# A transformer block on one core: the last of seven products moved to the free half of another PSUM bank, and two matmuls of the down projection cut in two

## The chip, the cores and the metric

The kernel runs on one core of a Trainium2 chip. A core has a matrix engine (TensorE; PE in the profile, and PEld for its weight loads), a vector engine (VectorE, DVE), a scalar engine (ScalarE, ACT), GpSimd (POOL), and the queue that issues most DMAs (SyncE, SP). Matmul results go to PSUM, eight banks of 512 float32 columns on 128 partitions; everything else on the chip lives in SBUF. The metric is the device time of one launch in microseconds.

## The reference

One layer of a hybrid encoder block over 512 positions of width 1024, in float32: an attention mixer with two head groups, a cross-attention into 256 memory tokens, and a SwiGLU feed-forward layer, each with an RMSNorm before and after. The change touches the feed-forward layer alone:

```
D_MODEL = 1024; SEQ = 512; D_FF = 2816

def swiglu(h, w_gate_up, w_down):
    g, u = jnp.split(h @ w_gate_up, 2, axis=-1)
    return (jax.nn.silu(g) * u) @ w_down
...
h = rms_norm(x, g_ffn_pre[l])
x = x + rms_norm(swiglu(h, w_gate_up[l], w_down[l]), g_ffn_post[l])
```

## The kernel before

**Three matmuls for one.** Each float32 operand is held as a high part and a low part. A product of two of them is three matmuls (`mm3`, lines 140 to 142): high by high, high by low, low by high. Each matmul has a weight load of its own, 128 rows by 128 columns, in front of it. The moving operand is 256 or 512 columns wide; in this text a 256-column matmul is one whose moving operand has 256 columns.

**Gate and up.** The 2816 columns of gate and of up are worked in blocks of 256 columns, alternately one of gate and one of up. There are 22 blocks; the first two are done with the end of cross-attention, and 20 follow in the loop over `u`. Three of these 20 multiply in the plain way (`eight`, 96 matmuls). The other 17 use a scheme in the manner of Strassen and Winograd: seven products of half-size blocks and some additions in place of eight products (`seven`, line 1116). One product (`product`, line 1063) is 4 times `mm3`, 12 matmuls of 256 columns, so a block of seven has 84 matmuls. All 256-column work of this stage forms one unbroken sequence on PE.

A block of seven takes four PSUM banks, called `p17`, `p26`, `p35` and `p4`. Gate blocks take three banks of the group "a" and the one bank "o"; up blocks take two banks "s" and two "t". A half bank (`left` or `right`, 256 columns) holds one product. In order, the seven products go to p17 left, p26 right, p35 left, p26 left, p4 left, p17 right and, once more, p26 left. VectorE combines them into `O` (the tile `G` for gate, `U` for up): line 1128 reads both halves of p26 after the fourth product, line 1129 reads p35, line 1134 reads p17 right, line 1135 reads p4 left, and line 1138 reads the seventh product. The seventh product overwrites p26 left, which line 1128 has to have read by then.

**Weights.** The weights arrive by DMA in tiles `fraw` (three buffers). VectorE adds blocks of them (`sums`, lines 929 to 932), ScalarE writes the high part into a ring (`ring_hi`, line 902), and VectorE writes the low part (`ring_lo`, line 903). The ring has two places for the first item of a block of seven and three for the other three items (`single`, `double`); `take` fills a place as soon as the products that used it are written down in the program. All of this and the combining of products share VectorE's and ScalarE's queues, whose order a scheduler fixes when the program is built.

**Down projection.** The output is worked in two halves of 512 columns (`half`). Four of the eleven blocks of the hidden dimension (`SEVEN`) are again done with seven products (`seven_products`, line 1242): 42 matmuls of 256 columns each, 168 in a row for the four blocks. The other blocks (`down`, line 1223) are matmuls of 512 columns. In half 0 the order is four blocks of 512 columns, the 168 matmuls of 256 columns, and blocks of 512 columns; in half 1 it is one block of 512 columns, the 168, and the rest. So each half has one 256-column stretch that begins and ends between 512-column matmuls. `mm` (line 1218) sends each operand pair to `mm3`.

Of the kernel before, what the change touches and what calls it, by code (L numbers as in the profile page):

```python
# [11 lines left out]
ALU = mybir.AluOpType  # L12
AX = mybir.AxisListType

P = 128
SEQ = 512
D = 1024
NT = SEQ // P
# [18 lines left out]
def hybrid_block_kernel(  # L37
# [20 lines left out]
    act, dve, pool, pe = nc.scalar, nc.vector, nc.gpsimd, nc.tensor  # L58
# [12 lines left out]
    def f32(ap):  # L71
        return ap.bitcast(F32)
# [66 lines left out]
    def mm3(dst, sh, sl, mh, ml, first, last):  # L139
        pe.matmul(dst, sh, mh, start=first, stop=False)  # L140
        pe.matmul(dst, sh, ml, start=False, stop=False)  # L141
        pe.matmul(dst, sl, mh, start=False, stop=last)  # L142
# [84 lines left out]
    with tc.tile_pool(name="mix", bufs=1, reuse_waits="tile") as bp:  # L227
# [114 lines left out]
        for t in range(NT):  # L342
# [3 lines left out]
                out=z[:, t, :], in0=acc0[t][:, 256:264], scalar=r, in1=gn[:, B_F : B_F + 8],  # L346
# [34 lines left out]
        for b in range(3):  # L381
            l = bp.tile([P, 2, SEQ], F32R, tag=f"L{b}", name=f"L{b}")
# [261 lines left out]
    with tc.tile_pool(name="cross", bufs=1, reuse_waits="tile") as cp:  # L644
# [12 lines left out]
        def quarter(name, dtype=F32R):  # L657
            serial[0] += 1
            return cp.tile([P, 1024], dtype, tag="q", name=f"{name}{serial[0]}", bufs=8)
# [5 lines left out]
        with later(-115):  # L665
            for c in range(4):
                hi, lo = unit()
                acc = bank("a")
                for b in range(2):
# [9 lines left out]
                    out=kT[:, 1, 2 * c : 2 * c + 2, :], in0=a3,  # L679
                    in1=f32(kT[:, 0, 2 * c : 2 * c + 2, :]), op=ALU.subtract,  # L680
# [4 lines left out]
        for half in range(2):  # L685
            hi, lo = unit()
            for t in range(NT):
                acc = bank("a")
                for k in range(4):
# [5 lines left out]
                    out=m, in0=acc, scalar=rs_g[1][:, t : t + 1], in1=m, op0=ALU.mult, op1=ALU.add  # L695
# [3 lines left out]
                if half:  # L699
                    r = small(1, "prs")  # L700
                    dve.scalar_tensor_tensor(
                        out=r, in0=mix_ms[:, 0, t : t + 1], scalar=EPS, in1=mix_ms[:, 1, t : t + 1],
# [4 lines left out]
                        out=mix[:, t, :], in0=mix[:, t, :], scalar=r, in1=xo[t], op0=ALU.mult, op1=ALU.add  # L707
# [35 lines left out]
        for h in range(4):  # L743
            for o in (oTh, oTl):
                t = quarter("oT").rearrange("p (k n) -> p k n", k=2)
                o += [t[:, 0], t[:, 1]]
        for h in range(4):
            hi, lo = unit()
            q = qq[:, h % 2]
            for b in range(2):  # L750
                acc = bank("a")
                cs = slice(b * P, (b + 1) * P)
                for k in range(KB):
# [3 lines left out]
                    out=q[:, 1, b, :], in0=acc, scalar=1.0 / 16.0, in1=f32(q[:, 0, b, :]),  # L757
# [3 lines left out]
            for i in range(0, NT, 2):  # L761
                s = bank("s")
                for j in range(2):
# [8 lines left out]
                    out=nm, in_=s.rearrange("p (j n) -> p j n", j=2), axis=AX.X, op=ALU.max, negate=True  # L772
# [9 lines left out]
                for j in range(2):  # L782
                    dve.tensor_scalar(
                        out=p[:, i + j, :], in0=p[:, i + j, :], scalar1=rs[:, j : j + 1],
# [11 lines left out]
            for b in range(2):  # L796
                acc = bank("o")
                cs = slice((2 * h + b) * P, (2 * h + b + 1) * P)
                for k in range(2):
# [6 lines left out]
                    out=oTl[2 * h + b], in0=acc, in1=f32(oTh[2 * h + b]), op=ALU.subtract  # L806
# [146 lines left out]
        SEVEN = (4, 5, 6, 7)  # L953
        DOWN = ((0, 1, 2, 3, 4, 5, 6, 7, 8, 9, 10), (0, 4, 5, 6, 7, 1, 2, 3, 8, 9, 10))
# [108 lines left out]
        def product(dst, w, b, first=True, last=True):  # L1063
            for k in range(4):
                mm3(dst, w[0][:, k, :], w[1][:, k, :], b[:, 0, k, :], b[:, 1, k, :], first and k == 0, last and k == 3)

        left, right = slice(0, 256), slice(256, 512)
# [22 lines left out]
        for b in range(2):  # L1090
# [5 lines left out]
        t1, t2, t3, t4 = (  # L1096
            wp.tile([P, 2, 4, 256], F32R, tag=tag, name=f"t{tag}", bufs=2) for tag in ("hi", "hi", "lo", "lo")
        )
# [14 lines left out]
        def twice(a):  # L1113
            return bass.AP(a.tensor, a.offset, [list(a.ap[0]), [0, 2], list(a.ap[-1])])

        def seven(O, tags, done):

            p17, p26, p35, p4 = (bank(tag) for tag in tags)
            v = cp.tile([P, 256], F32, tag="v", name="v", bufs=2)
            (a11,) = take()  # L1120
            product(p17[:, left], a11, b11)
            act.copy(v, p17[:, left])
            ((h, l),) = take()
            product(p26[:, right], (h[:, 0], l[:, 0]), t2)
            product(p35[:, left], (h[:, 1], l[:, 1]), b22)
            ((h, l),) = take()
            product(p26[:, left], (h[:, 0], l[:, 0]), b21)
            dve.tensor_tensor(out=O[:, 0], in0=halves(p26), in1=twice(v), op=ALU.add)
            dve.tensor_tensor(out=O[:, 1, 0], in0=p35[:, left], in1=O[:, 0, 1], op=ALU.add)
            done(0, 0)  # L1130
            product(p4[:, left], (h[:, 1], l[:, 1]), t4)
            ((h, l),) = take()
            product(p17[:, right], (h[:, 0], l[:, 0]), t3)
            dve.tensor_tensor(out=O[:, 1, 1], in0=p17[:, right], in1=O[:, 0, 1], op=ALU.add)
            dve.tensor_tensor(out=O[:, 0, 1], in0=p4[:, left], in1=O[:, 1, 1], op=ALU.add)
            done(0, 1)
            product(p26[:, left], (h[:, 1], l[:, 1]), t1)
            dve.tensor_tensor(out=O[:, 1], in0=twice(p26[:, left]), in1=O[:, 1], op=ALU.add)
            done(1, 0)
            done(1, 1)  # L1140

# [14 lines left out]
        for u in range(1, FB // 2):  # L1156
# [4 lines left out]
            dst = hidden(u)  # L1161
# [49 lines left out]
        for half, tail in enumerate((2, 3)):  # L1211
# [3 lines left out]
            p1, p5, p7, p6 = (bank(tag) for tag in (("s", "s", "t", "t"), ("a", "a", "a", "o"))[half])  # L1215
            begun = set()

            def mm(bank_, to, lhs, rhs, end=False):
                first = id(bank_) not in begun
                begun.add(id(bank_))  # L1220
                mm3(bank_[:, to], lhs[0], lhs[1], rhs[0], rhs[1], first, end)

            def down(t, i, w, end=False, parts=(slice(0, 512),)):
                ts = slice(t * P, (t + 1) * P)
                for to in parts:
                    for j in range(2):
                        k = 2 * i + j
                        mm(
                            accs[t], to, (gh[k][:, ts], gl[k][:, ts]), (w[0][:, j, to], w[1][:, j, to]),
                            end and j == 1 and to is parts[-1],  # L1230
                        )
# [10 lines left out]
            def seven_products(u, last):  # L1242
                (w,) = take()
                block(p1, u, 0, w, 0, last)
                block((0, 0), u, 1, w, 1)
                block((0, 1), u, 5, w, 2)
                (w,) = take()
                block(p5, u, 6, w, 0, last)
                block(p7, u, 4, w, 1, last)
                block(p6, u, 3, w, 3, last)  # L1250
                block((2, 0), u, 2, w, 2)
# [13 lines left out]
            body = DOWN[half][: FB // 2 - tail]  # L1265
            for i in body:
                if i in SEVEN:
                    seven_products(i, i == SEVEN[-1])
                    if half == 0 and i == SEVEN[0]:
                        spare = cp.tile([P, 4160], F32R, tag="vm", name="latev")  # L1270
                        late(8, spare)
                        late(9, spare[:, 2048:])
                    if half == 0 and i == SEVEN[1]:
                        late(10, cp.tile([P, 2112], F32R, tag="pt", name="latep"))
                    if i == SEVEN[-1]:
                        gather()
                    continue
                (w,) = take()
                if half == 0 and i < 4:
                    late_seven(SEVEN[i])  # L1280
                for t in range(NT):
                    down(t, i, w)
            ends = take(tail)
            for t in range(NT):
# [11 lines left out]
                else:  # L1296
# [8 lines left out]
                    for hf in range(2):  # L1305
                        c2 = slice(hf * 512, (hf + 1) * 512)
                        dve.scalar_tensor_tensor(
                            out=yd[:, t, c2], in0=(yd[:, t, c2], gained)[hf], scalar=r, in1=xr[:, t, c2],
# [58 lines left out]
```

## Time and profile before

| | |
|---|---|
| median of three runs | 787.18 us (786.44 to 787.55) |
| the profiled execution | 786.29 us, of which the span of the trace is 783.9 us |
| granted clock of PE | 0.998 of full speed |
| PE busy | 763.0 us of 783.9 |
| DVE busy | 592.1 us |
| ACT busy | 426.7 us |
| gate and up, from the first ring weights to the down projection | 462.5 to 660.5 us |
| 256-column stretch of down, half 0 | 682.2 to 702.0 us |
| 256-column stretch of down, half 1 | 723.8 to 743.6 us |

The profile takes one execution. The record of one matmul overlaps those of its neighbours, since matmuls are pipelined; how fast PE goes is read from the distance of their starts. The two microseconds and a half between span and time lie outside the trace.

### The profile page before, as it was taken

Reading aid. Unit: us, or ns where it says so; the run is one execution under the profiler, and the core shown is the slowest. Engines: PE = TensorE matmul, PEld = TensorE weight load, DVE = VectorE, ACT = ScalarE, POOL = GpSimd, SP = SyncE. Lnnn points to the kernel's source line nnn. Section 1 sums busy time; section 2 is a strip of 40 time slices with the busy share of each in tenths; the row PEclk is TensorE's granted clock in tenths of the full one; section 3 lists DMA queues with packets and bytes.
Section 4 is the critical chain, followed back from the end, with each engine's and each line's share of the span. In section 5 each row is a group of like instructions: output and inputs, shape, how many; then the busy total and the mean of one; then the engine's idle time right before and its main releaser. Section 6 shows DMA issues by size and latency. Waiting matters only on the chain.

```text
span 783.9 us, 12757 instructions
## 1 busy us (share of the span) xinstructions
PE 763.0 (97%) x4958; PEld 679.9 (87%) x4958; DVE 592.1 (76%) x1073; ACT 426.7 (54%) x774; POOL 70.8 (9%) x110
## 2 busy tenths in 40 slices
PE   8999999999999999999999999999999999999996
PEld 8887788888778888877778899999999999898985
DVE  6567889879887588545663778998899999986626
ACT  7358888757875348444553635545354446543411
POOL 6001231110321101000001100000000000000001
PEclk9999999999999999999999999999999999999999
DMA  7342112422322724421350202332433332241402
GB/s 245 83 132 55 54 55 68 137 68 78 109 68 90 275 106 162 133 75 60 108 174 15 81 28 81 108 109 81 135 109 108 108 110 105 84 159 57 138 23 108
DMA packets 60747, 80.04 MB, mean 102 GB/s; under 512 B 2704, under 2 KB 43664, under 8 KB 60688
## 3 DMA queue, kind: packets, MB, share of 16 engines
q1 hardware_dynamic: 59264, 74.49, 29.4%
q0 software_dynamic: 1280, 4.72, 1.8%
q8 instruction: 39, 0.64, 0.3%
q14 instruction: 20, 0.16, 0.1%
q10 hardware_dynamic: 144, 0.02, 0.0%
HBM read 77.13 MB, written 2.10 MB: 101 GB/s over the span
## 4 chain that ended last, share of the span: by engine, by line
PE 73%; DVE 11%; ACT 6%; issue 4%; DMA 3%; POOL 2%; SPq 0%; DVEq 0%; POOLq 0%; ACTq 0%
PE ps_a L141 14%; PE ps_a L142 14%; PE ps_a L140 14%; PE ps_s L140 4%; PE ps_s L141 4%; PE ps_s L142 4%; DVE ring_lo L903 3%; PE ps_t L534 2%; DMA raw<-in_dram 2%; PE ps_t L141 2%; PE ps_t L140 2%; PE ps_t L142 2%; PE ps_o L543 2%; PE ps_o L140 1%; PE ps_s L515 1%
## 5 line engine op out<-in xcount | busy, mean ns | idle before, releaser
L902 ACT CAST ring_hi<-fraw 128x1024 fp32r<-128x1024 f32 (+1 forms) x62 | 57.5, 932 | 64.6 <-PE ps_t L142 17.6
L126 DVE TENSOR_TENSOR lo<-raw,hi 128x1024 fp32r<-128x1024 f32 x56 | 68.2, 1223 | 22.2 <-ACT hi L125 21.9
L903 DVE TENSOR_TENSOR ring_lo<-fraw,ring_hi 128x1024 fp32r<-128x1024 f32 (+1 forms) x62 | 66.4, 1074 | 21.7 <-ACT ring_hi L902 21.5
L142 PE MATMUL ps_a<-hTh,lo 128*128 128x512 f32 x192 | 76.8, 400 | 0.6 <-DVE lo L126 0.6
L140 PE MATMUL ps_a<-hTh,hi 128*128 128x512 f32 x192 | 75.9, 395 | 0.2 <-ACT hi L125 0.2
L141 PE MATMUL ps_a<-hTl,hi 128*128 128x512 f32 x192 | 76.0, 396 | 0.0
L125 ACT CAST hi<-raw 128x1024 fp32r<-128x1024 f32 x56 | 57.8, 1048 | 24.0 <-PE ps_a L141 15.2
L902 ACT CAST ring_hi<-sums 128x1024 fp32r<-128x1024 f32 x34 | 35.7, 1050 | 48.7 <-PE ps_a L141 20.0
L903 DVE TENSOR_TENSOR ring_lo<-sums,ring_hi 128x1024 fp32r<-128x1024 f32 x34 | 41.4, 1219 | 3.4 <-ACT ring_hi L902 3.4
L142 PEld LDWEIGHTS ps_a<-hTh,lo 128*128 128x128 f32 x192 | 36.1, 188 | 7.3 <-DVE lo L126 1.0
L141 PEld LDWEIGHTS ps_a<-hTl,hi 128*128 128x128 f32 x192 | 36.1, 188 | 6.4
L140 PEld LDWEIGHTS ps_a<-hTh,hi 128*128 128x128 f32 x192 | 36.2, 188 | 6.1 <-ACT hi L125 0.4
L529 ACT ACTIVATE p<-p,nm 128x128 f32<-128x128 f32 (+1 forms) x64 | 36.1, 564 | 8.4 <-DVE nm L519 7.6
L140 PE MATMUL ps_a<-b,ring_hi 128*128 128x256 f32 x140 | 39.0, 279 | 0.0
L141 PE MATMUL ps_a<-b,ring_hi 128*128 128x256 f32 x140 | 38.9, 278 | 0.0
L142 PE MATMUL ps_a<-b,ring_lo 128*128 128x256 f32 x140 | 38.9, 278 | 0.0
L140 PE MATMUL ps_s<-b,ring_hi 128*128 128x256 f32 x128 | 35.6, 278 | 0.0
L141 PE MATMUL ps_s<-b,ring_hi 128*128 128x256 f32 x128 | 35.6, 278 | 0.0
L142 PE MATMUL ps_s<-b,ring_lo 128*128 128x256 f32 x128 | 35.6, 278 | 0.0
L536 ACT CAST pth<-ps_t 128x128 fp32r<-128x128 f32 (+1 forms) x64 | 27.1, 425 | 14.6 <-PE ps_t L534 13.8
L537 DVE TENSOR_TENSOR ptl<-ps_t,pth 128x128 fp32r<-128x128 f32 (+1 forms) x64 | 30.7, 486 | 5.0 <-ACT pth L536 3.6
L534 PE MATMUL ps_t<-ident,p 128*128 128x128 f32 x160 | 28.1, 275 | 1.1 <-DVE p L531 0.8
(528 smaller groups left out, 2618.0 us busy)
## 6 DMA issues: line engine op xcount, KB each, us to landing
raw<-in_dram SPq DMA_DIRECT2D x64, 512.0 KB, 3.7
fraw<-in_dram SPq DMA_DIRECT2D x62, 512.0 KB, 3.5
cb<-in_dram SPq DMA_DIRECT2D x8, 256.0 KB, 2.6
xo<-in_dram POOLq DMA_DIRECT2D x4, 512.0 KB, 5.3
out_dram<-yd SPq DMA_DIRECT2D x8, 256.0 KB, 2.0
rawv<-in_dram SPq DMA_DIRECT2D x3, 520.0 KB, 6.2
xt<-in_dram SPq DMA_DIRECT2D x3, 512.0 KB, 7.0
gb<-in_dram POOLq DMA_DIRECT2D x3, 512.0 KB, 5.0
```

The lines of the kernel that those rows point to most:

```text
L125: act.copy(hi[:, j : j + n, :], raw)
L126: dve.tensor_tensor(out=lo[:, j : j + n, :], in0=raw, in1=f32(hi[:, j : j + n, :]), op=ALU.subtract)
L140: pe.matmul(dst, sh, mh, start=first, stop=False)
L141: pe.matmul(dst, sh, ml, start=False, stop=False)
L142: pe.matmul(dst, sl, mh, start=False, stop=last)
L529: act.activation(p[:, :n], p[:, :n], AF.Exp, bias=nm, scale=-1.0, accum_out=sm)
L534: pe.transpose(tp[:, k * P : (k + 1) * P], p[:, k * P : (k + 1) * P], ident)
L536: act.copy(span(ph, i), t3)
L537: dve.tensor_tensor(out=span(pl, i), in0=t3, in1=f32(span(ph, i)), op=ALU.subtract)
L543: pe.matmul(acc[:, a:], v[:, k, vh, :], m[:, k * PTS + a : k * PTS + SEQ], start=k == 0 and m is ph, stop=k == NT - 1 and m is pl,)
L902: act.copy(h2, v)
L903: dve.tensor_tensor(out=l2, in0=v, in1=f32(h2), op=ALU.subtract)
```

## The change

In `seven`, the seventh product goes to p4 right instead of p26 left. Nothing else uses p4 right. The line that issues it now stands ahead of the VectorE line that reads p4 left. The last VectorE line reads p4 right in place of p26 left.

In the down projection, two matmuls, of all those that `mm` issues, have their third part (low by high) cut into two matmuls over a part of the columns each, with the same weights, so each of the two has its own weight load. In half 0 it is the first matmul of the 256-column stretch, cut into 128 and 128 columns. In half 1 it is the last-but-one operand pair of 512 columns ahead of the stretch, cut into 384 and 128 columns; three matmuls of 512 columns stand between it and the stretch.

```
@@ in seven
             dve.tensor_tensor(out=O[:, 1, 1], in0=p17[:, right], in1=O[:, 0, 1], op=ALU.add)
+            product(p4[:, right], (h[:, 1], l[:, 1]), t1)
             dve.tensor_tensor(out=O[:, 0, 1], in0=p4[:, left], in1=O[:, 1, 1], op=ALU.add)
             done(0, 1)
-            product(p26[:, left], (h[:, 1], l[:, 1]), t1)
-            dve.tensor_tensor(out=O[:, 1], in0=twice(p26[:, left]), in1=O[:, 1], op=ALU.add)
+            dve.tensor_tensor(out=O[:, 1], in0=twice(p4[:, right]), in1=O[:, 1], op=ALU.add)
             done(1, 0)
             done(1, 1)
@@ in the down projection
+            cuts = []
+
             def mm(bank_, to, lhs, rhs, end=False):
                 first = id(bank_) not in begun
                 begun.add(id(bank_))
-                mm3(bank_[:, to], lhs[0], lhs[1], rhs[0], rhs[1], first, end)
+                if not cuts:
+                    mm3(bank_[:, to], lhs[0], lhs[1], rhs[0], rhs[1], first, end)
+                    return
+                cut, dst = cuts.pop(), bank_[:, to]
+                pe.matmul(dst, lhs[0], rhs[0], start=first, stop=False)
+                pe.matmul(dst, lhs[0], rhs[1], start=False, stop=False)
+                for part in (slice(0, cut), slice(cut, to.stop - to.start)):
+                    pe.matmul(dst[:, part], lhs[1], rhs[0][:, part], start=False, stop=end)
...
                 if i in SEVEN:
+                    if half == 0 and i == SEVEN[0]:
+                        cuts.append(P)
                     seven_products(i, i == SEVEN[-1])
...
                 for t in range(NT):
+                    if half and t == NT - 1 and DOWN[1].index(i) + 1 == DOWN[1].index(SEVEN[0]):
+                        cuts.append(384)
                     down(t, i, w)
```

On PE, the start of the seventh product in the second up block that uses seven products; `ps_s_5187` is that block's p17, `ps_s_5188` its p26, `ps_t_5190` its p4, and `tlo` and `thi` are sums of the moving operand. Before:

```order
L142 MATMUL ps_s_5187<-tlo,ring_lo 128x256
L140 MATMUL ps_s_5188<-thi,ring_hi 128x256 [waits DVE_49]
L141 MATMUL ps_s_5188<-thi,ring_hi 128x256
L142 MATMUL ps_s_5188<-thi,ring_lo 128x256
L140 MATMUL ps_s_5188<-thi,ring_hi 128x256
```

and now:

```order
L142 MATMUL ps_s_5187<-tlo,ring_lo 128x256
L140 MATMUL ps_t_5190<-thi,ring_hi 128x256
L141 MATMUL ps_t_5190<-thi,ring_hi 128x256
L142 MATMUL ps_t_5190<-thi,ring_lo 128x256
L140 MATMUL ps_t_5190<-thi,ring_hi 128x256
```

PE's wait for VectorE ahead of the seventh product is gone; the order on PE is the same.

On DVE, the combining in the same block. Before:

```order
L1128 TENSOR_TENSOR U<-ps_s_5188,v 128x512 [waits PE_49]
L1129 TENSOR_TENSOR U<-ps_t_5189,U 128x256 [waits DVE_49]
L903 TENSOR_TENSOR ring_lo<-fraw_5196,ring_hi 128x4x2x128 [waits PE_49,Activation_49]
L1134 TENSOR_TENSOR U<-ps_s_5187,U 128x256 [waits PE_49]
L1135 TENSOR_TENSOR U<-ps_t_5190,U 128x256 [waits DVE_49]
L1138 TENSOR_TENSOR U<-ps_s_5188,U 128x512 [waits DVE_49,PE_49]
L903 TENSOR_TENSOR ring_lo<-sums,ring_hi 128x1024 [waits Activation_49]
```

and now:

```order
L1128 TENSOR_TENSOR U<-ps_s_5188,v 128x512 [waits PE_49]
L1129 TENSOR_TENSOR U<-ps_t_5189,U 128x256 [waits DVE_49]
L903 TENSOR_TENSOR ring_lo<-fraw_5196,ring_hi 128x4x2x128 [waits PE_49,Activation_49]
L1134 TENSOR_TENSOR U<-ps_s_5187,U 128x256 [waits PE_49]
L1136 TENSOR_TENSOR U<-ps_t_5190,U 128x256 [waits DVE_49,PE_49]
L1138 TENSOR_TENSOR U<-ps_t_5190,U 128x512 [waits DVE_49]
L903 TENSOR_TENSOR ring_lo<-sums,ring_hi 128x1024 [waits Activation_49]
```

The wait for the seventh product has moved one VectorE instruction forward: the line that reads p4 left (1135 before, 1136 now) waits for PE too. In later blocks the scheduler also exchanges this pair with neighbouring `sums` and `ring_lo` operations on VectorE, and some casts on ScalarE with each other; the instructions are the same.

On PE, the cut ahead of the 256-column stretch of half 1, now (`g` is the hidden operand of the 512-column block, `latex` that of the first block of seven products; before, there was one matmul of 512 columns in the place of the two of line 1230):

```order
L1227 MATMUL ps_t_7623<-ring_hi,g_4828 128x512
L1228 MATMUL ps_t_7623<-ring_lo,g_4828 128x512
L1230 MATMUL ps_t_7623<-ring_hi,g_4829 128x384
L1230 MATMUL ps_t_7623<-ring_hi,g_4829 128x128
L140 MATMUL ps_t_7623<-ring_hi,g_4828 128x512
L141 MATMUL ps_t_7623<-ring_lo,g_4828 128x512
L142 MATMUL ps_t_7623<-ring_hi,g_4829 128x512
L140 MATMUL ps_a_7624<-ring_hi,latex_7120 128x256 [waits DVE_49,Activation_49]
```

One instruction more on PE in each half; nothing else moves there.

## The prediction, made before the changed kernel was run

> **What bounds the kernel now.** I read the page first, then the windows of the stages that the change touches, then single matmuls at the places where the pace changes, then the waits.
>
> ```profile
> span 783.9 us, 12757 instructions
> PE 763.0 (97%) x4958; PEld 679.9 (87%) x4958; DVE 592.1 (76%) x1073; ACT 426.7 (54%) x774; POOL 70.8 (9%) x110
> PE 73%; DVE 11%; ACT 6%; issue 4%; DMA 3%; POOL 2%; SPq 0%; DVEq 0%; POOLq 0%; ACTq 0%
> ```
>
> PE is busy for nearly the whole span and has 73% of the chain of waits. So in the touched stages two things count: how far apart the starts of matmuls are, and where PE waits. The windows (PE, PEld, DVE, ACT, POOL, each busy with its count) show the first:
>
> ```profile
> 465.00:520.00 55.00, 55.00 (x469) 55.00 (x468) 50.77 (x65) 27.72 (x38) 0.00 (x0) 1.00 0.29 87
> 535.00:600.00 65.00, 65.00 (x576) 65.00 (x575) 59.24 (x84) 30.07 (x47) 0.00 (x0) 1.00 0.37 116
> 631.00:639.00 8.00, 8.00 (x71) 8.00 (x70) 7.76 (x11) 4.29 (x8) 0.00 (x0) 1.00 0.29 84
> 641.00:660.00 19.00, 19.00 (x170) 19.00 (x169) 15.85 (x26) 11.62 (x20) 0.00 (x0) 1.00 0.25 85
> 664.00:682.00 18.00, 18.00 (x81) 14.90 (x80) 17.86 (x34) 7.11 (x9) 0.57 (x1) 1.00 0.37 118
> 683.00:702.00 19.00, 19.00 (x163) 19.00 (x163) 14.80 (x19) 10.99 (x14) 0.00 (x0) 1.00 0.36 120
> 725.00:743.00 18.00, 18.00 (x155) 18.00 (x154) 11.99 (x16) 7.64 (x11) 0.00 (x0) 1.00 0.38 128
> ```
>
> PE is busy throughout in all seven, the granted clock is 1.00, and the 256-column matmuls still run at two paces. A count includes two or three matmuls that only reach over an edge, since a record is 0.28 us long: 55 us by 466.6 is 117.9 ns, 65 by 573.6 is 113.3, 19 by 160.6 is 118.3, 18 by 152.6 is 118.0. Exact paces come from the starts of the same product, 84 matmuls apart, in a block at each pace:
>
> ```profile
> 483.62 0.28 PE L140 MATMUL ps_a<-b,ring_hi 128*128 128x256 f32 x1
> 493.51 0.28 PE L140 MATMUL ps_s<-b,ring_hi 128*128 128x256 f32 x1
> ...
> 564.02 0.28 PE L140 MATMUL ps_a<-b,ring_hi 128*128 128x256 f32 x1
> 573.54 0.28 PE L140 MATMUL ps_s<-b,ring_hi 128*128 128x256 f32 x1
> ```
>
> 9.89 by 84 is 117.7 ns (slow) and 9.52 by 84 is 113.3 ns (fast). I use 117.78 and 113.33, a difference of 4.45 ns, which the long windows agree with. Both stretches of down (683 to 702, 725 to 743) are slow; gate and up are slow up to 522, fast after that, and slow again in the eight microseconds from 631. So the pace does not belong to the line or to the operands. It changes only where PE's rhythm is disturbed. The first such place is at 455:
>
> ```profile
> 453.98 1.22 DVE L865 TENSOR_TENSOR b<-f,b 128x1024 fp32r<-128x1024 f32 x1
> 455.12 0.28 PE L140 MATMUL ps_a<-b,gate_w 128*128 128x256 f32 x1
> 455.24 0.40 PE L141 MATMUL ps_a<-b,gate_w 128*128 128x256 f32 x2
> 455.47 0.28 PE L142 MATMUL ps_a<-b,gate_w 128*128 128x256 f32 x1
> 455.59 0.28 PE L140 MATMUL ps_a<-b,gate_w 128*128 128x256 f32 x1
> ```
>
> The second matmul of the 0.40 us row needs what line 865 wrote. Line 865 ends at 455.20, just as PE gets there; the distance of starts goes from 0.113 to 0.12 there and is 0.118 afterwards, for 66 us. The places after it are the waits before the seventh product:
>
> ```profile
> PEld ps_a L140 <- DVE G L1128: 0.9, 1, 0.9
> PEld ps_s L140 <- DVE U L1128: 0.6, 2, 0.3
> ...
> 521.66 0.28 PE L142 MATMUL ps_s<-tlo,ring_lo 128*128 128x256 f32 x1
> 522.07 0.39 PE L140 MATMUL ps_s<-thi,ring_hi 128*128 128x256 f32 x1
> 522.29 0.28 PE L141 MATMUL ps_s<-thi,ring_hi 128*128 128x256 f32 x1
> ...
> 600.81 0.39 PE L140 MATMUL ps_s<-thi,ring_hi 128*128 128x256 f32 x1
> ...
> 610.47 0.38 PE L140 MATMUL ps_a<-thi,ring_hi 128*128 128x256 f32 x1
> ...
> 620.37 0.38 PE L140 MATMUL ps_s<-thi,ring_hi 128*128 128x256 f32 x1
> ...
> 630.03 0.39 PE L140 MATMUL ps_a<-thi,ring_hi 128*128 128x256 f32 x1
> ...
> 640.03 0.29 PE L140 MATMUL ps_s<-thi,ring_hi 128*128 128x256 f32 x1
> ...
> 660.45 0.40 PE L140 MATMUL ps_a<-ring_hi,g 128*128 128x512 f32 x1
> ```
>
> At 522 the wait costs 0.29 us beyond the pace, and 0.11 more because the second matmul starts 0.22 after the first. The pace after it is fast. There are seven such disturbances, each at a seventh product, where the record of the first matmul is longer than the usual 0.28: at 522.1, after the wait of 0.9 us (532.6), and at the five rows from 600.81 on. Six left the pace fast, and 630.03 left it slow. All waits together are 1.5 us.
>
> **Part by part: the seventh product.** It takes away that wait, everywhere. No matmul is added and no bank is short: p4's next use is a whole gate and up pair later. What it adds is on VectorE: line 1136 now waits until the seventh product has ended, 1.36 us (12 by 113.3 ns) after the sixth, with ring fills queued behind it. Bounds: nothing where VectorE is late anyway, and about 0.45 us a block where it is not, since line 1138 waited for the same matmul before and only line 1136's 0.42 us moves behind it. Who waits for that is PE, through the ring:
>
> ```profile
> 598.94 1.22 DVE L903 TENSOR_TENSOR ring_lo<-sums,ring_hi 128x1024 fp32r<-128x1024 f32 x1
> 600.07 0.68 DVE L1128 TENSOR_TENSOR U<-ps_s,v 128x512 f32<-128x512 f32 x1
> ...
> 603.66 0.28 PE L140 MATMUL ps_a<-thi,ring_hi 128*128 128x256 f32 x1
> ```
>
> The fill that ends at 600.16 is first used at 603.66: VectorE may be 3.5 us later than now before PE waits. The longest wait at a seventh product is 0.9 us, so with the wait gone, PE should meet no other. That is the cover for the 0.45 us.
>
> With no wait left, nothing resets the pace after 455. So this part is worth either of two sums. From 521.78 (where the seventh product would have started) to 660.45 are 138.67 us and 1200 matmuls (12 of this product, 13 blocks of 84, one of 96). At the fast pace they take 136.00 us, -2.67; at the slow one 141.33, +2.66. From 455.59 to 521.78 are 66.19 us, 562 matmuls at 117.78 ns, slow now; if they are fast, -2.50. Fast throughout is -5.17, slow throughout +2.66.
>
> **The cuts.** A matmul of 128 columns is bounded by its weight load. Eight transposes of that size, and a 256-column stretch entered from 512-column matmuls whose rhythm was disturbed, look like this:
>
> ```profile
> 302.09 1.03 PE L166 MATMUL ps_t<-ident,mix 128*128 128x128 f32 x8
> ...
> 330.55 0.39 PE L140 MATMUL ps_a<-hTh,hi 128*128 128x512 f32 x1
> 330.78 0.40 PE L141 MATMUL ps_a<-hTl,hi 128*128 128x512 f32 x1
> 331.01 0.28 PE L142 MATMUL ps_s<-kT,qq 128*128 128x256 f32 x1
> ...
> 331.60 0.28 PE L141 MATMUL ps_s<-kT,qq 128*128 128x256 f32 x1
> 331.71 0.39 PE L142 MATMUL ps_s<-kT,qq 128*128 128x256 f32 x2
> 331.94 0.28 PE L140 MATMUL ps_s<-kT,qq 128*128 128x256 f32 x1
> ```
>
> The first row gives 0.11 us each (1.03 less one record's 0.28, by 7). In half 0 a matmul of 0.118 becomes two of 0.11, +0.10; in half 1 one of 0.227 (18 us by 79.3) becomes 0.17 (three quarters of it) and 0.11, +0.05. For an unsettled rhythm behind each I add 0.03, an estimate from the 0.22 at 522.29. If the stretch comes out fast, 168 by 4.45 ns is -0.75 each. In the fence the 512-column starts are 0.23 apart, unsettled, and four matmuls into the 256-column run the distance is 0.113 (331.60 to 331.94 is three); the two stretches of down, entered from settled matmuls 0.227 apart, are slow. So the cuts give between +0.2 (both stay slow) and -1.3 (both fast). I take -1.3, the row it is nearest to. Nothing hides PE there: it is busy throughout, so all of it reaches the end.
>
> The Trainium skill, "TensorE: Matmul & The Clock Gate", section "Back-to-back issue gap", gives one distance per column count, 256/2.4 + 2.5 = 109 ns here, and no second pace. The trace disagrees: 113.3 and 117.8 at granted clock 1.00. By it the cuts would cost the 0.2 and bring nothing, and the seventh product its waits alone; that is the last rival below.
>
> **The sum.** -5.17 - 1.28 = -6.45 us on the profiled execution's 786.29 gives 779.8; its time lies 0.9 under the median of 787.18, and against that it is 780.7. I forecast 780.8.
>
> **Rivals.**
>
> Slow throughout (other side). The slip at 455.2 lies ahead of all that is changed and may come again; before, the wait at 522 ended the slow pace, and now nothing does. Then gate and up are +2.66, and with the cuts at -1.28 the sum is +1.38: 788.6 against the median, 790.0 if the cuts fail as well. It decides once some 1440 of the 1762 matmuls from 455.6 on are slow (6.4 us by 4.45 ns). For it: the same few instructions precede it, and the four times before lie within 1.3 us. Against it: the slip is the size of a few nanoseconds on VectorE, and of eight known disturbances six ended fast.
>
> In between. The pace changes once on the way, at a late ring fill, or VectorE binds for a while (7.76 of 8.00 us busy from 631): half of the gain, 783 to 785.5.
>
> The wait only moves. VectorE is the chain's 11%; if its lateness adds up past 3.5 us, PE waits at the ring for what it no longer waits for at the seventh product: the 1.5 us come back, pace and all, 785.9 to 787.2. It takes eight blocks in a row of the full 0.45 us. Against it is VectorE's 59.24 of 65 us: 5.8 us idle in seven blocks.
> The Trainium skill, "PSUM — Partial Sum Buffer", section "Terms", speaks for this rival: it has TensorE writing and VectorE reading one bank at once as an error, so p4's bank is shut to VectorE for the whole seventh product. No run here shows such an access.
>
> The pace belongs to the place, not to the disturbance: waits, restarts and 0.2 for the cuts alone, -1.5 - 0.7 + 0.2, 785.2. The equal operands at both paces speak against it.
>
> **Chances and range.** Fast throughout 0.45, slow throughout 0.30, in between 0.15, the wait moves 0.05, place 0.05. The likeliest's own range is 779.5 to 783. Over all cases 779.5 to 788.7 leaves out the upper half of the slow case and little below. A change of under 0.2% (1.6 us) cannot be told from none here. Faster is the first, third and last case: 0.65. The slow case lies at that bound, half inside: 0.15 slower, and with the moved wait 0.20 the same.
>
> **What would show it.** Step one: no wait of PE for line 1128, and no other in its place, between 462 and 660. Step two: windows in gate and up at 113.3 ns; at 117.8 from 455 on the slow rival has come. Step three: both stretches of down at 113.3 ns, 19.04 us for 168 matmuls in place of 19.79. The prediction is wrong if the slip at 455 repeats, or if a cut leaves its stretch slow.

## The result, and the profile after

The changed kernel took 780.66 us (median of four runs, 780.19 to 781.50) against 786.97 us for the kernel before in the same session (four runs, 786.44 to 787.55): a ratio of 0.9918, with a 95% interval of 0.9901 to 0.9934. The forecast was 780.8. Two later sessions with twelve runs each gave 0.9944 (0.9915 to 0.9972) and 0.9955 (0.9925 to 0.9985), because the runs of the changed kernel then fell in two groups, one at 779.1 to 783.3 and one at 787.2 to 789.4 us. What these groups are turned out to be the main finding.

The profiled execution of the first session took 780.42 us, 5.87 less than the one of before; the span is 5.4 less, and the remaining 0.5 lies outside the trace. The page of after has these three lines in place of those that the prediction began with:

```profile
span 778.5 us, 12763 instructions
PE 758.2 (97%) x4960; PEld 675.8 (87%) x4960; DVE 591.2 (76%) x1073; ACT 426.3 (55%) x774; POOL 70.8 (9%) x110
PE 76%; DVE 9%; ACT 7%; issue 3%; DMA 3%; POOL 2%; SPq 0%; DVEq 0%; POOLq 0%; ACTq 0%
```

PE's busy time fell by 4.8 us although it issues two matmuls more, and VectorE's share of the chain of waits fell from 11% to 9%. The windows of the touched stages show where this comes from (start and end in us, length, then PE, PEld, DVE, ACT and POOL busy with their counts, granted clock, DMA share, GB/s):

```profile
465.00:520.00 55.00, 55.00 (x488) 55.00 (x487) 52.88 (x68) 28.70 (x39) 0.00 (x0) 1.00 0.28 87
535.00:600.00 65.00, 65.00 (x576) 65.00 (x575) 60.33 (x88) 30.99 (x46) 0.00 (x0) 1.00 0.38 117
641.00:655.00 14.00, 14.00 (x126) 14.00 (x125) 12.86 (x20) 8.96 (x17) 0.00 (x0) 1.00 0.34 111
660.00:676.00 16.00, 16.00 (x72) 13.25 (x71) 15.93 (x30) 5.97 (x8) 0.57 (x1) 1.00 0.40 145
679.00:688.00 9.00, 9.00 (x82) 9.00 (x81) 7.88 (x13) 6.20 (x9) 0.00 (x0) 1.00 0.18 60
721.00:738.00 17.00, 17.00 (x153) 17.00 (x152) 11.71 (x17) 7.29 (x9) 0.00 (x0) 1.00 0.42 138
```

From 465 to 520 there are 488 matmuls where before there were 469, at the same granted clock of 1.00. Less the two or three that only reach over an edge, that is 113.3 ns in place of 117.9. The second window was fast before and is unchanged. Both stretches of the down projection (the last two rows) are now fast as well, at about 113 ns: 9 us by 79.5 and 17 by 150.5.

The slip at 455 did come again:

```profile
452.21 0.28 PE L142 MATMUL ps_a<-b,gate_w 128*128 128x256 f32 x1
...
454.27 1.22 DVE L865 TENSOR_TENSOR b<-f,b 128x1024 fp32r<-128x1024 f32 x1
...
455.50 0.43 PE L141 MATMUL ps_a<-b,gate_w 128*128 128x256 f32 x2
455.77 0.28 PE L142 MATMUL ps_a<-b,gate_w 128*128 128x256 f32 x1
...
456.24 0.28 PE L140 MATMUL ps_a<-b,gate_w 128*128 128x256 f32 x1
```

PE is 0.26 us later here than before (455.50 against 455.24), in a part of the program that the change doesn't touch. Line 865 ends at 455.49, and the two steps from 455.50 to 455.77 take 0.27 us, 0.04 more than two at the fast pace. Four steps to 456.24 take 0.47, a little uneven, and what follows is fast. The down projection starts at 655.59, 4.86 us before its old 660.45; with the 0.26, gate and up have gained 5.12 us.

Between 455 and 775 the only wait of PE and its weight loads is a new one, in the first stretch of the down projection:

```profile
PE ps_s L141 <- DVE ring_lo L903: 0.5, 1, 0.5
PEld ps_s L141 <- DVE ring_lo L903: 0.7, 1, 0.7
```

In the timeline it stands at 689, behind VectorE's early splitting of operands (`latev`, `latep`) and two ring fills:

```profile
684.58 0.69 DVE L979 TENSOR_TENSOR fraw<-fraw 128x512 f32<-128x512 f32 x1
685.19 1.23 DVE L1200 TENSOR_TENSOR latep<-gf,latep 128x1024 fp32r<-128x1024 f32 x1
686.33 0.42 DVE L980 TENSOR_TENSOR fraw<-fraw 128x256 f32<-128x256 f32 x1
...
688.54 1.23 DVE L903 TENSOR_TENSOR ring_lo<-fraw,ring_hi 128x1024 fp32r<-128x1024 f32 x1
```

```profile
689.07 0.28 PE L140 MATMUL ps_s<-ring_hi,latehi 128*128 128x256 f32 x1
689.82 0.38 PE L141 MATMUL ps_s<-ring_lo,latehi 128*128 128x256 f32 x1 [0.48 <-DVE ring_lo L903]
690.04 0.28 PE L142 MATMUL ps_s<-ring_hi,latehi 128*128 128x256 f32 x1
```

From 689.07 to 689.82 is 0.75 us for one step of 0.113, and the next step is 0.22. VectorE is busy for 15.93 of the 16 us from 660 to 676: PE now comes 4.86 us earlier to fills for which VectorE has no time to spare.

### The profile page after: what moved, and what is told of

Same layout as the page of the kernel before. It is cut to its first block, busy times and chain, and to the rows that moved or that the text cites. A ratio compares the mean times of both kernels' runs of the same rounds, so it can differ in the third digit from the quotient of the medians.

```text
span 778.5 us, 12763 instructions
## 1 busy us (share of the span) xinstructions
PE 758.2 (97%) x4960; PEld 675.8 (87%) x4960; DVE 591.2 (76%) x1073; ACT 426.3 (55%) x774; POOL 70.8 (9%) x110
## 4 chain that ended last, share of the span: by engine, by line
PE 76%; DVE 9%; ACT 7%; issue 3%; DMA 3%; POOL 2%; SPq 0%; DVEq 0%; POOLq 0%; ACTq 0%
PE ps_a L141 14%; PE ps_a L142 14%; PE ps_a L140 14%; PE ps_s L141 4%; PE ps_s L140 4%; PE ps_s L142 4%; PE ps_t L140 2%; PE ps_t L142 2%; PE ps_t L141 2%; PE ps_t L534 2%; PE ps_o L140 2%; PE ps_o L141 2%; PE ps_o L142 2%; DMA raw<-in_dram 2%; PE ps_o L543 2%
```

## The experiments

Except where it says so, the times are medians, each compared with the kernel before in the same session.

**One part alone.** The first keeps the edit of `seven` and drops the cuts; the second does the reverse.

> The seventh product's move alone, no cut in the down projection. Theory (the pace of 256-column matmuls is set by the last disturbance and then kept): gate and up run at 113.3 ns from 456 on without a wait, -5.0 us; both stretches of down stay at 117.8 ns; ring fill L903 still a little late in half 0 of down, +0.3. About 782.2 us, ratio 0.994. Rival (the pace belongs to the place, only the waits go): 1.5 us of waits and 0.7 of restarts, 784.8 us, ratio 0.997, slow windows at 465 to 520.

> The two cuts in the down projection alone, the seventh product as before. Theory: both stretches of down at 113.3 ns, 0.75 us each less about 0.05 to 0.1 for each cut, -1.35 us: 785.6 us, ratio 0.998; gate and up as before, slow to 522 and with the waits for L1128. Rival (the pace belongs to the place): stretches stay at 117.8 ns and the cuts cost 0.2, 787.2 us, ratio 1.000.

The seventh product alone: 788.52 us, ratio 0.9979 (0.9953 to 1.0006). The cuts alone: 786.63 us, ratio 0.9984 (0.9964 to 1.0004). Neither tells anything as a median. But the twelve runs of the first are three at 781.4 to 782.4 and nine at 787.9 to 789.9, and none between. That is the forecast of fast throughout for this part and the one of slow throughout, 7 us apart, from one program. The profiled execution is one of the three:

```profile
490.00:520.00 30.00, 30.00 (x267) 30.00 (x267) 29.15 (x44) 16.40 (x25) 0.00 (x0) 1.00 0.34 105
535.00:600.00 65.00, 65.00 (x576) 65.00 (x576) 60.05 (x86) 31.12 (x48) 0.00 (x0) 1.00 0.40 121
```

Both windows are at the fast pace. That left a question: does the pace in gate and up explain the 7 us, and is it set at one place?

**Setting the pace.** Both kernels are the changed one with eight unused 512-column matmuls into the bank "o" ahead of the first gate block of seven products. In the second of them the fifth of the eight is cut in two.

```
+            if u == 2:
+                spin = bank("o")
+                wide = bt[0][:, 0, 0, 0:2, :].rearrange("p k n -> p (k n)")
+                for j in range(8):
+                    for part in (slice(0, 512),):        # second kernel, j == 4: slice(0, 384), slice(384, 512)
+                        pe.matmul(spin[:, part], bt[0][:, 0, 0, 0, :P], wide[:, part], start=j == 0, stop=j == 7)
```

> The changed kernel with eight matmuls of 512 columns, whose result nobody reads, ahead of the first block of seven products, so that the 1524 matmuls of 256 columns from there on follow settled matmuls of 512 columns, as both stretches of down did before. Theory: they all run at 117.8 ns, +6.8 us, and the eight cost 1.8; the late ring fill in half 0 of down is covered again, -0.7: 788.5 us. Rival (in gate and up the pace is fast unless a semaphore comes late, whatever stands ahead): only the eight, 782.4 us.

> As the kernel with the eight matmuls of 512 columns, but the fifth of them is cut into 384 and 128 columns, with three of 512 behind it, as in half 1 of down. Theory: the one cut makes all 1524 matmuls behind it run at 113.3 ns: 782.5 us, 6 us under the kernel without the cut, though it has one instruction more. Rival: the cut changes nothing, the same time as without it.

Whole: 789.38 us, ratio 1.0014 (0.9997 to 1.0031), ten runs, all from 787.9 to 790.4. With the cut: 782.98 us, ratio 0.9937 (0.9909 to 0.9964), five runs, all from 782.1 to 785.6. One window of each, whole first:

```profile
535.00:600.00 65.00, 65.00 (x554) 65.00 (x553) 57.69 (x84) 29.48 (x46) 0.00 (x0) 1.00 0.36 113
```

```profile
535.00:600.00 65.00, 65.00 (x576) 65.00 (x575) 59.52 (x86) 30.54 (x46) 0.00 (x0) 1.00 0.38 117
```

PE is busy for all of the 65 us in both, the clock is the same, and there are 554 matmuls in one and 576 in the other: 117.9 and 113.3 ns. One matmul cut in two, with no other difference, is worth 6.4 us. So the pace is a state that PE keeps for 1500 matmuls and more (1524 of 256 columns follow here), and the place and operands don't decide it.

**The changed kernel again.** The same program, with more runs.

> The changed kernel as it is, with more runs. Its matmuls up to the first cut of the down projection are those of the kernel with the seventh product alone, whose twelve runs fell in two groups, three at 781.4 to 782.4 us and nine at 787.9 to 789.9. Theory (the pace from 456 us on is drawn at the short wait at 455.6, and nothing draws it again before the first cut): two groups here too, one at 780.2 to 781.5, the other later by up to 1760 x 4.44 ns = 7.8 us less the 0.75 us wait at 689 that a later TensorE does not meet, that is at 787 to 788.5; nothing between 782.5 and 786. Rival (the cuts of the down projection, or anything else of the whole change, make the fast pace sure): one group, 780 to 782.

782.02 us, ratio 0.9944 (0.9915 to 0.9972): eight runs at 780.1 to 782.6 and four at 787.4 to 788.9, and none between, as the theory had it, though the early ones reach 1.1 us past its 781.5. The profiled execution was one of the four:

```profile
451.69 0.38 PE L141 MATMUL ps_a<-b,gate_w 128*128 128x256 f32 x1
451.91 0.28 PE L142 MATMUL ps_a<-b,gate_w 128*128 128x256 f32 x1
...
455.33 0.40 PE L141 MATMUL ps_a<-b,gate_w 128*128 128x256 f32 x2
455.56 0.28 PE L142 MATMUL ps_a<-b,gate_w 128*128 128x256 f32 x1
...
663.20 0.39 PE L140 MATMUL ps_a<-ring_hi,g 128*128 128x512 f32 x1
...
773.65 0.28 PE L140 MATMUL ps_t<-ring_hi,latev 128*128 128x256 f32 x1
```

and its window from 535 to 600 has the slow count:

```profile
535.00:600.00 65.00, 65.00 (x554) 65.00 (x554) 57.35 (x82) 28.87 (x45) 0.00 (x0) 1.00 0.37 112
```

The place was wrong, though. From the matmul behind the 0.38 us record to the row of two ahead of the slip are 29 steps in both profiles. They take 3.42 us here (451.91 to 455.33) and took 3.29 in the early one (452.21 to 455.50): 117.9 and 113.4 ns. So the slow pace was already there at 452, PE came to line 865 late enough to find its result, and no slip followed (455.33 to 455.56 is 0.23 us for two steps, against 0.27 in the early profile). It then held up to the down projection, which begins at 663.20 instead of 655.59, and PE has no wait at all from 455 to 690. The profile of the last session's run, a late one too, shows the same. Together with the first session and the last one below, 28 runs of the changed kernel are 19 in the early group (mean 780.9) and 9 in the late group (mean 788.0).

**What sets it.** Two kernels were made for their profile alone: the changed one with short sequences of unused matmuls ahead of the blocks, all in one execution. In their edits a tuple is one matmul, with its parts:

```
u=2, 4, 6, 8: eight of (512)        u=5: four of (512), (256, 256), three of (512)
u=3: (128, 128)   u=7: (192, 64)    u=9: four of (512), (128, 384), three of (512)
```

> The changed kernel with unused matmuls into a spare bank ahead of the gate and up blocks of u = 2 to 9: eight whole 512-column matmuls at u = 2, 4, 6 and 8; one 256-column matmul in parts of 128 and 128 at u = 3; the fifth of eight 512-column ones in parts of 256 and 256 at u = 5; one 256-column matmul in parts of 192 and 64 at u = 7; the fifth of eight in parts of 128 and 384 at u = 9. One profile, read by the spacing of the 256-column matmuls that follow (about 168 to the next place). Theory (the pace is a state that a whole 512-column run leaves slow and a part with fewer columns sets fast): 117.78 ns after u = 2, 4, 6, 8 and 113.33 ns after u = 3, 5, 7, 9. Rival a (512-column runs keep the pace that they meet): 113.33 ns everywhere after u = 3. Rival b (only a part of 128 columns or fewer resets it): 117.78 ns after u = 5. Rival c (the reset needs the 512-column run around it): 117.78 ns after u = 3 and u = 7. No time is forecast; the added matmuls take some 11 us.

Each window lies behind one place; these are u = 2, 3, 5, 6, 7 and 9:

```profile
487.00:504.00 17.00, 17.00 (x147) 17.00 (x146) 15.09 (x23) 8.17 (x13) 0.00 (x0) 1.00 0.31 94
507.00:524.00 17.00, 17.00 (x147) 17.00 (x145) 15.62 (x23) 9.45 (x14) 0.00 (x0) 1.00 0.27 85
551.00:568.00 17.00, 17.00 (x153) 17.00 (x152) 13.59 (x20) 6.32 (x10) 0.00 (x0) 1.00 0.32 100
573.00:590.00 17.00, 17.00 (x146) 17.00 (x145) 14.40 (x21) 7.82 (x13) 0.00 (x0) 1.00 0.31 95
593.00:610.00 17.00, 17.00 (x146) 17.00 (x146) 16.54 (x25) 7.85 (x13) 0.00 (x0) 1.00 0.33 104
637.00:654.00 17.00, 17.00 (x147) 17.00 (x146) 14.85 (x21) 7.28 (x11) 0.00 (x0) 1.00 0.30 94
```

In 17 us 153 matmuls are the fast pace and 146 or 147 the slow one. Only the cut in 256 and 256 set the fast pace; 128 and 128, 192 and 64, and 128 and 384 did not, each tried at one place. Eight whole matmuls made it slow again (fourth row). So the theory was half wrong: a cut doesn't set the pace for being short. Nor is 128 and 128 without effect everywhere: it is the cut of half 0 of the down projection, behind matmuls of 512 columns, and there the stretch behind it is fast, but for the wait described above, in all eleven profiles with the cuts. The second such kernel looked for the shortest sequence that does.

```
u=2: four of (512), (384, 128), three of (512)     u=3, 5, 7, 9: eight of (512)
u=4: two of (512), (384, 128), (512)    u=6: (512), (384, 128), (512)
u=8: (384, 128)                         u=10: two of (512), (256, 256), (512)
```

> The changed kernel with other unused matmuls ahead of the gate and up blocks, to find the shortest sequence that sets the fast pace: at u = 2 four whole 512-column matmuls, one in parts of 384 and 128, three whole ones; at u = 4 two whole, one 384 and 128, one whole; at u = 6 one whole, one 384 and 128, one whole; at u = 8 one 384 and 128 alone; at u = 10 two whole, one 256 and 256, one whole; eight whole ones at u = 3, 5, 7 and 9. Theory (it is the shift that a 384 and 128 cut leaves between weight load and matmul that counts, and some whole 512-column matmuls must stand ahead of it): 113.33 ns after u = 2 and u = 4, 117.78 ns after the whole ones and after u = 8, u = 6 and u = 10 open. Rival (any 384 and 128 cut does it, as 192 and 64 or 128 and 384 do not): 113.33 ns after u = 8 too. No time is forecast; the added matmuls take some 11 us.

Behind u = 2, 4, 6, 8 and 10:

```profile
490.00:506.00 16.00, 16.00 (x144) 16.00 (x143) 14.68 (x22) 7.71 (x13) 0.00 (x0) 1.00 0.32 100
531.00:548.00 17.00, 17.00 (x147) 17.00 (x146) 13.72 (x21) 9.01 (x13) 0.00 (x0) 1.00 0.22 71
575.00:591.00 16.00, 16.00 (x143) 16.00 (x143) 14.77 (x23) 7.96 (x13) 0.00 (x0) 1.00 0.32 99
616.00:632.00 16.00, 16.00 (x144) 16.00 (x143) 15.72 (x24) 8.05 (x13) 0.00 (x0) 1.00 0.34 105
656.50:674.00 17.50, 17.50 (x151) 17.50 (x150) 12.80 (x19) 9.59 (x19) 0.00 (x0) 1.00 0.26 87
```

Fast, slow (147 in 17 us), fast, fast (143 or 144 in 16 us), slow (151 in 17.5 us). The rival was right on u = 8: a single matmul in parts of 384 and 128, without whole ones around it, does it. The same cut between two whole ones and one (u = 4) does not, and neither does 256 and 256 there (u = 10), which had worked among seven whole ones. No rule comes out that tells from the columns alone which cut works; it has to be tried.

**Taking the draw out.** That shortest sequence, put into the changed kernel between the gate and the up block of u = 1 at about 472 us, and into the kernel with the seventh product alone:

```
             dst = hidden(u)
+            if u == 1:
+                spin = bank("o")
+                wide = bt[0][:, 0, 0, 0:2, :].rearrange("p k n -> p (k n)")
+                for part in (slice(0, 384), slice(384, 512)):
+                    pe.matmul(spin[:, part], bt[0][:, 0, 0, 0, :P], wide[:, part], start=True, stop=True)
```

> The changed kernel with one unused 512-column matmul in parts of 384 and 128 columns between the gate and the up block of u = 1, at about 472 us: the shortest sequence that has set the fast pace. Theory (the pace from 456 us on is drawn at the wait at 455.6 and kept until something sets it): one group. Where the draw was fast, 780.4 us plus some 0.3 for the two parts; where it was slow, 0.64 us more, for about 144 matmuls between 456 and 473 at 4.44 ns each: all runs between 780.3 and 783, none at 787 or above, median near 781.3. Rival a (the two parts set the fast pace only from the slow one, and can turn a fast one slow): two groups again, 781 and 787 to 789. Rival b (what differs between the groups is not this pace): the groups of the changed kernel, 780 to 782.6 and 787.4 to 788.9, both 0.3 us later.

> The kernel before with the seventh product changed, no cuts in the down projection, and the same unused matmul in two parts at about 472 us. Theory (as above; the two stretches of 168 256-column matmuls in the down projection then run at 117.78 ns, but for the part of the first behind the wait at 690, which restarts fast): one group, 1.1 us above the kernel with the cuts, the difference between the starts of the last 34 matmuls in the profiles of the two (768.05 and 766.92 us): median near 782.4. Rival (both stretches gain their full 0.75 us less the cost of the cut, as the prediction had it): 1.3 us above. Rival (the cuts are hidden behind VectorE's late work): 0.4 us or less above.

With the cuts: 782.48 us, ratio 0.9910 (0.9886 to 0.9933), six runs, 780.2 to 783.1. Without: 782.46 us, ratio 0.9915 (0.9893 to 0.9938), six runs, 780.9 to 784.4. Both are one group; against the seventh product alone, whose runs were nine late of twelve, the two parts took the late group away. (In the profiled execution of each, the pace at 472 was fast already; that the two parts turn a slow pace fast is seen at u = 8 above.) The second expectation failed: it had the kernel without cuts 1.1 us later, and the medians are equal. Each set spreads over about 3 us, so six runs don't tell 1 us. The median of the first is also 1.2 us above the 781.3 expected of it, and its profile has a wait that I had not reckoned with, at 617, for ScalarE's copy:

```profile
PE ps_s L140 <- ACT v L1122: 0.9, 1, 0.9
```

What the cuts are worth is read from the profiles, below.

**The new wait.** The subtraction that makes `latep`, 1.23 us on VectorE ahead of the late ring fill, was given to GpSimd, in the kernel with the cuts and the two parts:

```
-            dve.tensor_tensor(out=l, in0=gf_views[u], in1=f32(h), op=ALU.subtract)
+            (pool if u == 10 else dve).tensor_tensor(out=l, in0=gf_views[u], in1=f32(h), op=ALU.subtract)
```

> The changed kernel with the unused matmul in two parts at about 472 us, and with one subtraction of the early splitting for the down projection (latep, 128 x 1024, 1.23 us on VectorE at 685.19 in the changed kernel) on GpSimd, which is otherwise idle there. Theory (TensorE's wait at 689 is for a ring fill that stands behind this subtraction on VectorE): the wait is gone, and the time from the first 512-column matmul of the down projection to the last 34 matmuls is 109.4 us, as in the four profiles whose TensorE came late enough, against 110.2 and 110.3 with the wait; median 0.75 us below the 782.48 us of the kernel with the two parts alone, near 781.7. Rival (GpSimd's work slows VectorE's, or another VectorE instruction is the late one): the wait stays at 0.5 us or more, and the time is the same as without.

783.01 us, ratio 0.9942 (0.9920 to 0.9963): no gain, and the wait of PE for the fill is still there, by the waits and then the timeline of this kernel. The time that was to fall is 111.44 us by the measure of the table below, against 111.38 and 111.23 without this change (the 109.4 of the expectation, counted from a matmul 1.1 us later, is 110.45 there):

```profile
PE ps_s L141 <- DVE ring_lo L903: 0.7, 1, 0.7
```

```profile
685.06 0.68 DVE L979 TENSOR_TENSOR fraw<-fraw 128x512 f32<-128x512 f32 x1
...
685.72 2.40 POOL L1205 TENSOR_TENSOR latep<-gf,latep 128x1024 fp32r<-128x1024 f32 x1 [22.48 <-ACT latep L1204]
...
685.78 2.62 DVE L980 TENSOR_TENSOR fraw<-fraw 128x256 f32<-128x256 f32 x1
688.44 0.43 DVE L981 TENSOR_TENSOR fraw<-fraw 128x256 f32<-128x256 f32 x1
```

The rival came true. GpSimd works from 685.72 to 688.12, and the VectorE instruction that starts at 685.78 takes 2.62 us where it took 0.42 before. It ends at 688.40, 0.28 us after GpSimd, so VectorE stood still for most of that time, and the 1.23 us saved became 2.2 us lost. The Trainium skill, "SBUF — State Buffer", section "Who interferes with whom", says this: a VectorE instruction with both inputs in SBUF and a GpSimd instruction that reads SBUF shut each other out for a whole instruction. The trace agrees.

This profile shows one thing more: the fast pace was lost at 634.17, by a matmul whose record is 0.30 us long and without a wait that the profile shows, and PE stayed slow up to the down projection (121 matmuls from 641 to 655, where the changed kernel had 126). So the two parts set the pace, but don't hold it against a later disturbance.

**Side by side.** The changed kernel and the one with the two parts, in one session:

> The changed kernel once more, beside the one with the unused matmul in two parts, on one chip. Theory (the pace is drawn at 455.6 in each execution and kept): runs at 780 to 782.6 and at 787 to 789 and none between 783.5 and 786.5, with 3 to 9 of 12 in the later group. Rival (the two groups seen before belong to the chip of that call): one group.

> The changed kernel with the unused matmul in two parts at about 472 us, beside the changed kernel on the same chip. Theory (the two parts set the fast pace whatever was drawn before): all runs between 780 and 784.5; the mean lies below the mean of the changed kernel by 7 us times the share of the latter's runs that are in the later group, less some 0.5 us. Rival (a fast pace can be turned slow there): runs at 787 and above.

The changed kernel: 782.56 us, ratio 0.9955 (0.9925 to 0.9985), seven runs at 779.1 to 783.3 and five at 787.2 to 789.4. With the two parts: 781.60 us, ratio 0.9934 (0.9911 to 0.9958), five runs, 780.4 to 783.7. The means are 783.7 and 781.9. Over all sessions 23 runs of kernels with the two parts at 472 us lie between 780.2 and 784.4, none later. That version does not beat the changed kernel's early group; it removes the late one. The two intervals overlap, so a lower median is not shown, only the missing group.

## Why the prediction was right, point by point

**The seventh product (-5.17).** Right in kind and size, for the early group against the profiled execution of before: no wait of PE for line 1128 and none in its place from 462 to 655, the fast pace throughout, and 5.12 us gained up to the down projection. That the pace is set by a disturbance and then kept was inferred from eight disturbances; the two kernels with eight unused matmuls show it. But 2.50 of the 5.17 are the slow pace up to 522 that this one execution of before had drawn, and nothing in the change ends that. The profile of the cuts alone, whose gate and up are those of before, was fast there (153 matmuls from 465 to 482, where before had 147) and slow from 600 to 659 instead (122 from 641 to 655, where before had 126). So the kernel before draws its pace too, and more than once on the way. Over the three sessions with the changed kernel, its 28 runs have a mean of 783.2 us and the 38 of the kernel before one of 787.3: on the mean the change is worth some 4 us, not 6.

**The rival of slow throughout.** It also came true, as 788.6 was forecast and 787.2 to 789.4 was measured in 9 of 28 runs. Here the prediction took for a question with one answer what is drawn anew in each execution. The first four runs happened to be early ones. It also put the decision at one place, the slip at 455. In the two late executions that were profiled, it had fallen at 452 and there was no slip. The kernel before and the two with eight unused matmuls, on the other hand, came to 455 fast and left it slow, so it can fall there too. Of the fourteen profiles of all kernels, four came to 455 slow and met no slip; ten came fast, and three of these left it slow. How a slip turns out was not settled. What the prediction said of the wait at 522 holds: it used to end a slow pace, and without it a slow pace lasts up to the down projection.

**The cuts (-1.28).** Right. The time from the first 512-column matmul of the down projection (line 140, `ps_a<-ring_hi,g`) to the first of the last 256-column ones (`ps_t<-ring_hi,latev`) is worked out from the two starts in each profile, as 773.65 - 663.20 in the one above:

| | cuts | wait at the ring fill | us |
|---|---|---|---|
| before (660.45 to 772.19) | no | no | 111.74 |
| changed, late group, two profiles | yes | no | 110.45, 110.44 |
| cuts alone | yes | no | 110.45 |
| eight unused matmuls, whole; with a cut | yes | no | 110.45, 110.44 |
| changed, early group (655.59 to 766.81) | yes | yes | 111.22 |
| two parts at 472, two profiles | yes | yes | 111.38, 111.23 |
| seventh product alone; with two parts | no | yes | 112.02, 112.31 |

111.74 less 110.45 is 1.29 us, in five profiles.

**The cover.** This step failed. The prediction looked for VectorE's slack in gate and up, found 3.5 us in the ring, and concluded that PE would meet no other wait. In gate and up that held in the profile of the changed kernel (one of the kernels with the two parts met 0.9 us at 617). But PE then came 4.86 us earlier to the down projection, and there the same VectorE was already busy for 17.86 of 18 us in a window that the prediction itself showed. 111.22 less 110.45 is 0.77 us given back. A PE that comes late, as in the late group, does not meet it. It is not its arrival alone, though: the kernel with eight unused matmuls and a cut begins the down projection at 658.03 and has the fill 0.23 us before it is needed, and the one with the wait at 617 begins at 657.98 and waits 0.7 us. What counts is how far VectorE is by then.

**The sum.** -6.45 was forecast on the profiled execution, and the span moved by -5.4: 0.77 for the wait, 0.26 for a PE that came later to 455, and 0.05 less in gate and up are the difference, to a few hundredths. With the 0.5 us outside the trace it is -5.87 on the profiled executions. The one of after lies 0.24 us under its median and the one of before 0.68 under its own, so the medians are 6.31 apart, and the median of before came out at 786.97 in place of 787.18. That these together lead to 780.66, beside a forecast of 780.8, is luck.

**Place, and the rule of one distance per column count.** Refuted: the same matmuls run at 113.3 or 117.8 ns in the same places, with PE busy throughout. The Trainium skill's "TensorE: Matmul & The Clock Gate", section "Back-to-back issue gap", gives the formula behind the prediction's 109 ns for the isolated gap of a matmul, says that in a stream the weight loads set the spacing too, and names no pace that is kept. By such a rule the cut among eight unused matmuls would have changed next to nothing; it changed 6.4 us.

## What to carry to other kernels

Where one engine is busy throughout at an unchanged clock, count its instructions per window and compare windows: a difference of 4% in the spacing of equal matmuls is time that no wait shows, and one cheap disturbance may set it for the rest of the stage. When runs of one program fall in groups, look at the head of a long undisturbed stretch, and give each group a profile before believing a median. A gain upstream is also an earlier arrival downstream: check the helper engines of the next stage, and measure before moving their work to GpSimd: here it held VectorE up for longer than the work had taken there.

## What was not expected of the hardware

- The pace of equal 256-column matmuls, 113.33 or 117.78 ns, held for up to 1760 of them in a row, and a single matmul in parts of 384 and 128 columns could change it, while parts of 128 and 128 or 192 and 64, each tried once between blocks of gate and up, did not. What in PE keeps this state is open. The last 36 of the program have a third distance, 119.8 ns, in all fourteen profiles, and nothing here tells why.
- Eight whole 512-column matmuls left the slow pace at each of the eight places of the two kernels where they stood; at four of them PE had come in fast.
- After a true wait the second matmul starts 0.22 us after the first (690.04 less 689.82).
- While GpSimd subtracted for 2.40 us, a VectorE instruction of 0.42 us took 2.62.
